# The last operations of the rope tables take a scratch unit of their own late in the first feed-forward stage; in the closing norm the third tile's weight and scale go to GpSimd and ScalarE

## The chip, the cores and the metric

The kernel runs on one core of one Trainium2 chip. Its engines are TensorE (PE in the profile, its weight loads PEld), VectorE (DVE), ScalarE (ACT), GpSimd (POOL) and SyncE (SP, which here only issues DMAs). Time is device microseconds of one execution; a result is the median of several.

## What is computed

One decoder layer over 512 tokens of width 1024, in float32: half a SwiGLU feed-forward, a mixing block, half a second SwiGLU, and a final RMSNorm.

```python
x = x + 0.5 * swiglu(rms_norm(x, ffn1_norm), ffn1_w_gate, ffn1_w_up, ffn1_w_down)
u = rms_norm(x, mix_norm) @ w_in           # [c_q | c_kv | k_rope | moba q | moba k | moba v]
a_out = mla_attention(c_q, c_kv, k_rope, positions, ...)    # uses apply_rope
b_out = moba_attention(mq, mk, mv, positions)
x = x + concat(a_out, b_out) @ w_out
x = x + 0.5 * swiglu(rms_norm(x, ffn2_norm), ffn2_w_gate, ffn2_w_up, ffn2_w_down)
return rms_norm(x, final_norm)

def apply_rope(x, pos):
    ang = pos[:, :, None, None] * 10000.0 ** (-arange(16) * 2 / 32)
    cos, sin = cos(ang), sin(ang)
    return concat([x1 * cos - x2 * sin, x1 * sin + x2 * cos])
```

[...] The feed-forward's inner width is 2816.

## The kernel before

**The matrix products.** A float32 product is made of three TensorE passes over operands that are split into a high and a low part. Every 512 KB piece of weights that a DMA brings into a buffer `raw` is split by one ACT operation (L251, the high part, a copy) and one DVE operation (L252, the low part, a difference) into two slots of the big tile `ar`. The gate and up matrices of a feed-forward are walked in pairs of column blocks (`pair`, L491). A pair is seven products of 24 matmuls each (`product`, L475, matmuls on L485), made by a scheme that trades one block product for sums of blocks; for this some pieces are first added or subtracted on DVE into the tile `sq` (L292, L295, L300) or in place (L297). Between the products ACT copies banks of PSUM to scratch (L495), and DVE adds them up and multiplies (L511, L513, L516, L517, L522, L524, L527); two silus run on ACT (L514, L525). The seventh product of a pair goes on in the bank that L516 reads after the fifth, so TensorE waits for L516 there. `pump` keeps the splitting up to four products ahead.

**Where the order comes from.** Each engine works its own queue strictly in order. The program is written once, and a scheduler decides the order in each engine's queue: it may put an instruction ahead of others where only data and buffers tie it. It works with durations of its own, not with measured ones. Two helpers shape it: `scr`, a scratch tile cut in nine units that `ualloc` and `ufreeit` hand out in rotation (an instruction that writes a unit must wait for the last reader of its earlier contents), and `aside`, a list of generators that `tick` advances by a step or two after each product, so that side work is written between the products.

**The rope tables.** `rope_tables` (L781) is such a generator, started with the fourth pair of the first feed-forward. It takes one scratch unit and cuts it in eight pieces of 64 columns (`a, t2, t1, n, p, q, z, y`). Some fifty small GpSimd operations on 128x64 (L794 to L849, each three-term step as L787 and L788) reduce the angles; L852 clamps the result in place in `a`. Then the generator idles until `state["late"]`, which is set for the last two of the pairs. After that come |a| on DVE (L857), pi/2 - |a| on GpSimd (L859), three sines on ACT (L862, L864 for the cosines, L866 for the sine of `a`), and a negated copy of the sines on GpSimd (L868). The tables are needed much later, in the mixing block (`c_evac`, L969, and `rope_transpose`, L874).

**The tail.** The last part is a loop over the four 128-token tiles `t` (L1423): the last products of the second half of the columns (L1417), the add to the residual on DVE (L1430), the sum of squares on ACT (L1434), an inverse square root in small steps (L1441 on ACT; L1442 to L1446 on DVE, giving `y`), and the scaling of both halves of the tile by `y` and the final norm's weights `gB`. The left half has been multiplied by its weights on GpSimd earlier (L1409) and is scaled on ACT (L1449); the right half is multiplied by both in one DVE operation (L1453). The last tile, t = 3, is cut in 384 and 128 columns, gets its weights early (L1439), and is scaled on DVE (L1451). SP issues the DMA of the right half (L1454), ACT's queue that of the left (L1455). The tiles `x_69` to `x_72` in the listings are t = 0 to 3.

Of the kernel before, what the change touches and what calls it, by code (L numbers as in the profile page):

```python
# [14 lines left out]
AF = mybir.ActivationFunctionType  # L15
OP = mybir.AluOpType
# [24 lines left out]
def _cut(v):  # L41
    b = np.array([v], np.float32).view(np.uint32) & 0xfffff000
    return float(b.view(np.float32)[0])
# [9 lines left out]
def layer_kernel(ctx, tc, xt, xtok, pos_row, pos_tok, gains, fin, consts, w, wc, out):  # L53
    nc = tc.nc
    V, A, G, T = nc.vector, nc.scalar, nc.gpsimd, nc.tensor
# [90 lines left out]
    def ualloc():  # L146
        u = ufree.popleft()
        return u, scr[:, u * 512:(u + 1) * 512]

    def ufreeit(u):  # L150
        ufree.append(u)
# [627 lines left out]
    blk = scr[:, (NU - 1) * 512:].rearrange("p (t c) -> p t c", t=4)  # L779

    def rope_tables():  # L781
        u, sc = ualloc()
        tl = [sc[:, i * 64:i * 64 + 64] for i in range(8)]
        a, t2, t1, n, p, q, z, y = tl

        def STT(o, a_, c, b_, op0, op1):
            G.tensor_scalar(y, a_, c, 1.0, op0=op0, op1=OP.mult)  # L787
            G.tensor_tensor(o, y, b_, op=op1)  # L788

        pf = sm[:, 68:72]  # L790
        V.tensor_copy(pf, pi)
        yield 1
        v3 = a.rearrange("p (t f) -> p t f", t=4)
        G.tensor_tensor(v3, pf[:, :, None].to_broadcast([128, 4, 16]),  # L794
                        cst[:, None, CINV - C0:CINV - C0 + 16].to_broadcast([128, 4, 16]), op=OP.mult)
        yield 1

        def reduce(x):
            G.tensor_scalar(n, x, 1.0 / _P, MAGIC, op0=OP.mult, op1=OP.add)
            yield 1  # L800
            G.tensor_scalar(n, n, -MAGIC, 1.0, op0=OP.add, op1=OP.mult)
            yield 1
            for c in (PI_A, PI_B, PI_C):
                STT(x, n, -c, x, op0=OP.mult, op1=OP.add)
                yield 1

        def fold(t, x, step):

            d = math.fmod(step, _P)
            d = d - _P if d > math.pi else d  # L810
            da = _cut(d)
            db = _cut(d - da)
            dc = d - da - db
            G.tensor_scalar(n, t, da / step / _P, MAGIC, op0=OP.mult, op1=OP.add)
            yield 1
            G.tensor_scalar(n, n, -MAGIC, 1.0, op0=OP.add, op1=OP.mult)
            yield 1
            G.tensor_scalar(x, t, da / step, 1.0, op0=OP.mult, op1=OP.mult)
            yield 1
            STT(x, n, -PI_A, x, op0=OP.mult, op1=OP.add)  # L820
            yield 1
            STT(x, t, db / step, x, op0=OP.mult, op1=OP.add)
            yield 1
            STT(x, n, -PI_B, x, op0=OP.mult, op1=OP.add)
            yield 1
            STT(x, t, dc / step, x, op0=OP.mult, op1=OP.add)
            yield 1
            STT(x, n, -PI_C, x, op0=OP.mult, op1=OP.add)
            yield 1

        m2, m1 = MAGIC * 2.0 ** 21, MAGIC * 2.0 ** 12
        G.tensor_scalar(t2, a, m2, 1.0, op0=OP.add, op1=OP.mult)
        yield 1
        G.tensor_scalar(t2, t2, -m2, 1.0, op0=OP.add, op1=OP.mult)
        yield 1
        G.tensor_tensor(a, a, t2, op=OP.subtract)
        yield 1
        G.tensor_scalar(t1, a, m1, 1.0, op0=OP.add, op1=OP.mult)
        yield 1
        G.tensor_scalar(t1, t1, -m1, 1.0, op0=OP.add, op1=OP.mult)  # L840
        yield 1
        G.tensor_tensor(a, a, t1, op=OP.subtract)
        yield 1
        yield from reduce(a)
        yield from fold(t1, p, 2.0 ** 12)
        yield from fold(t2, q, 2.0 ** 21)
        G.tensor_tensor(p, p, q, op=OP.add)
        yield 1
        G.tensor_tensor(a, a, p, op=OP.add)  # L849
        yield 1  # L850
        yield from reduce(a)
        G.tensor_scalar(a, a, 3.1415925, -3.1415925, op0=OP.min, op1=OP.max)  # L852
        yield 1

        while not state["late"]:
            yield 1
        V.scalar_tensor_tensor(z, a, -1.0, a, op0=OP.mult, op1=OP.max)  # L857
        yield 1
        G.tensor_scalar(z, z, -1.0, math.pi / 2, op0=OP.mult, op1=OP.add)  # L859
        yield 1  # L860
        z3 = z.rearrange("p (t f) -> p t f", t=4)
        A.activation(blk[:, :, 64:80], z3, AF.Sin)  # L862
        yield 1
        A.activation(blk[:, :, 80:96], z3, AF.Sin)  # L864
        yield 1
        A.activation(blk[:, :, 112:128], v3, AF.Sin)  # L866
        yield 1
        G.tensor_scalar(blk[:, :, 96:112], blk[:, :, 112:128], -1.0, 1.0, op0=OP.mult, op1=OP.mult)  # L868
        yield 1
        G.memset(blk[:, :, 0:64], 1.0)  # L870
        yield 1
        ufreeit(u)
# [8 lines left out]
    def dist_tables():  # L881
# [30 lines left out]
        for i in range(4):  # L912
# [10 lines left out]
            yield 1  # L923

    gate_up(c_f1, c_s1, start_mid0, start_mid1, rope_tables)
    down(c_d1, 8)
    close_part()
# [471 lines left out]
    gB = tabs[:, 0:1024]  # L1399
# [7 lines left out]
    for t in range(4):  # L1407
        xs = X[t][:, 0:512]
# [6 lines left out]
    def tail_mm(c, t, n):  # L1415
        a, b = parts[t][n]
        ts = slice(t * 128, t * 128 + 128)  # L1417
        ws = slice(512 + a, 512 + b)
        mm3(banks[acc[t][n]][:, 0:b - a], hi_(hT[c])[:, ts], lo_(hT[c])[:, ts],
            whi(c)[:, ws], wlo(c)[:, ws], t == 3 and c == last[0], c == last[-1],  # L1420
            skip_group_check=True)

    for t in range(4):  # L1423
        u, xg = ualloc()
        v = v0[:, t:t + 1]
        for n, (a, b) in enumerate(parts[t]):
            for c in last:
                tail_mm(c, t, n)
            xs = X[t][:, 512 + a:512 + b]
            V.scalar_tensor_tensor(xs, banks[acc[t][n]][:, 0:b - a], rh[:, t:t + 1], xs,  # L1430
                                   op0=OP.mult, op1=OP.add)
            uj, junk = ualloc()
            s1 = ss[:, 2 * t + n:2 * t + n + 1]
            A.activation(junk[:, 0:b - a], xs, AF.Square, accum_out=s1)  # L1434
            ufreeit(uj)
            if n + 1 < len(parts[t]):
                V.scalar_tensor_tensor(v, s1, 1.0 / D, v, op0=OP.mult, op1=OP.add)
            if t == 3:
                V.tensor_tensor(xg[:, a:b], xs, gB[:, 512 + a:512 + b], op=OP.mult)  # L1439
        w1, w2, y, z = tv[:, t:t + 1], tv[:, 4 + t:5 + t], rstd[:, t:t + 1], tt[:, t:t + 1]  # L1440
        A.activation(w1, s1, AF.Sqrt, scale=1.0 / D, bias=v)  # L1441
        V.scalar_tensor_tensor(w2, s1, 1.0 / D, v, op0=OP.mult, op1=OP.add)  # L1442
        V.tensor_scalar(w2, w2, -0.5, None, op0=OP.mult)
        V.reciprocal(y, w1)
        V.scalar_tensor_tensor(z, y, y, w2, op0=OP.mult, op1=OP.mult)
        V.scalar_tensor_tensor(y, z, 1.5, y, op0=OP.add, op1=OP.mult)  # L1446
        o = out[t * 128:t * 128 + 128, :]
        xs = X[t][:, 0:512]
        A.activation(xs, xs, AF.Copy, scale=y)  # L1449
        if t == 3:  # L1450
            V.tensor_scalar(xg, xg, y, None, op0=OP.mult)  # L1451
        else:
            V.scalar_tensor_tensor(xg, X[t][:, 512:1024], y, gB[:, 512:1024], op0=OP.mult, op1=OP.mult)  # L1453
        nc.sync.dma_start(o[:, 512:1024], xg)  # L1454
        nc.scalar.dma_start(o[:, 0:512], xs)  # L1455
# [88 lines left out]
```

## Time and profile before

| | |
|---|---|
| median of 3 runs | 953.11 us (951.67 to 954.19) |
| the profiled execution | 952.19 us, span 950.4 us, mean granted TensorE clock 0.989 |
| PE busy | 920.2 us, 97% |
| PEld busy | 838.1 us, 88% |
| DVE busy | 748.6 us, 79% |
| ACT busy | 517.4 us, 54% |
| POOL busy | 116.7 us, 12% |

The profile is of one execution. Its time, 952.19 us, holds the span from the first to the last instruction and 1.8 us around it. A row of a timeline gives the start in us from the span's start, the duration, the engine, the line, the operation, what is written and read, and in brackets the idle time before it with what ended it. In the rows of groups, "busy, mean ns" stand behind the bar. A sequencer's row (SPq, ACTq) is the issue of a DMA. `scr`, `sm`, `ar`, `sq`, `raw`, `bank`, `x`, `tabs` are the tiles; `tabs` holds `gB` in the tail.

### The profile page before, as it was taken

Reading aid. Unit: us, or ns where it says so; the run is one execution under the profiler, and the core shown is the slowest. Engines: PE = TensorE matmul, PEld = TensorE weight load, DVE = VectorE, ACT = ScalarE, POOL = GpSimd, SP = SyncE. Lnnn points to the kernel's source line nnn. Section 1 sums busy time; section 2 is a strip of 40 time slices with the busy share of each in tenths; the row PEclk is TensorE's granted clock in tenths of the full one; section 3 lists DMA queues with packets and bytes.
Section 4 is the critical chain, followed back from the end, with each engine's and each line's share of the span. In section 5 each row is a group of like instructions: output and inputs, shape, how many; then the busy total and the mean of one; then the engine's idle time right before and its main releaser. Section 6 shows DMA issues by size and latency. Waiting matters only on the chain.

```text
span 950.4 us, 15102 instructions
## 1 busy us (share of the span) xinstructions
PE 920.2 (97%) x5901; PEld 838.1 (88%) x5901; DVE 748.6 (79%) x1090; ACT 517.4 (54%) x832; POOL 116.7 (12%) x173
## 2 busy tenths in 40 slices
PE   8993999999999999999999999999999999999997
PEld 6993999999988888998787888899999999988886
DVE  6984989879988956445688887689798879988845
ACT  7643544545636525455787865655455544735524
POOL 2053000000000000011756730000000000000001
PEclk9997999999999999999999999999999999999999
DMA  9420433224603424132434362123233323610302
GB/s 329 174 89 24 133 112 112 90 91 152 220 5 100 118 89 138 62 126 72 152 121 152 125 195 98 45 69 109 90 93 127 114 89 112 221 67 26 109 0 89
DMA packets 38088, 105.41 MB, mean 111 GB/s; under 512 B 4480, under 2 KB 11264, under 8 KB 38016
## 3 DMA queue, kind: packets, MB, share of 16 engines
q1 hardware_dynamic: 37008, 102.61, 33.2%
q10 hardware_dynamic: 1008, 1.84, 0.5%
q8 instruction: 46, 0.75, 0.3%
q14 instruction: 26, 0.21, 0.1%
HBM read 90.40 MB, written 2.10 MB: 97 GB/s over the span
## 4 chain that ended last, share of the span: by engine, by line
PE 46%; ACT 2%; DVE 1%; POOL 1%; DMA 1%; issue 0%; ACTq 0%; SPq 0%; DVEq 0%; POOLq 0%
PE bank L485 21%; PE bank L326 7%; PE bank L328 7%; PE bank L327 7%; PE bank L1190 2%; PE bank L1172 1%; POOL scr L1143 1%; ACT scr L1135 1%; DMA ext<-scr 0%; PE bank L402 0%; ACT ar L251 0%; DMA ar<-scr 0%; DVE ext L1176 0%; ACT ar L1175 0%; POOL ext L1259 0%
## 5 line engine op out<-in xcount | busy, mean ns | idle before, releaser
L485 PE MATMUL bank<-ar 128*128 128x256 f32 x3360 | 406.6, 284 | 16.6 <-DVE scr L516 16.0
L485 PEld LDWEIGHTS bank<-ar 128*128 128x128 f32 x3360 | 405.2, 193 | 17.7 <-DVE scr L516 16.4
L251 ACT ACTIVATE ar<-raw 128x1024 fp32r<-128x1024 f32 (+3 forms) x182 | 177.0, 982 | 155.3 <-issue 45.5
L326 PE MATMUL bank<-ar 128*128 128x512 f32 (+4 forms) x664 | 255.3, 385 | 2.6 <-ACT ar L251 2.2
L328 PE MATMUL bank<-ar 128*128 128x512 f32 (+4 forms) x664 | 253.7, 382 | 0.0
L327 PE MATMUL bank<-ar 128*128 128x512 f32 (+4 forms) x664 | 253.6, 382 | 0.0
L252 DVE TENSOR_TENSOR ar<-raw,ar 128x1024 fp32r<-128x1024 f32 (+2 forms) x164 | 192.0, 1181 | 53.9 <-ACT ar L251 35.8
L326 PEld LDWEIGHTS bank<-ar 128*128 128x128 f32 x664 | 124.8, 188 | 25.9 <-ACT ar L251 2.6
L328 PEld LDWEIGHTS bank<-ar 128*128 128x128 f32 x664 | 125.1, 188 | 23.3
L327 PEld LDWEIGHTS bank<-ar 128*128 128x128 f32 x664 | 125.2, 188 | 22.4 <-DVE ar L390 0.2
L251 ACT ACTIVATE ar<-sq 128x1024 fp32r<-128x1024 f32 x62 | 65.6, 1058 | 77.4 <-DVE sq L295 27.1
L252 DVE TENSOR_TENSOR ar<-sq,ar 128x1024 fp32r<-128x1024 f32 x62 | 75.6, 1220 | 26.8 <-ACT ar L251 26.8
L1409 POOL TENSOR_TENSOR x<-x,tabs 128x512 f32<-128x512 f32 x4 | 5.2, 1288 | 353.6 <-ACT scr L354 353.6
L1143 POOL TENSOR_SCALAR scr<-scr,sm 128x128 f32<-128x128 f32 (+1 forms) x64 | 41.1, 662 | 41.4 <-DVE sm L1140 40.5
L617 DVE SCALAR_TENSOR_TENSOR x<-bank,sm,x 128x512 f32<-128x512 f32 x37 | 27.0, 747 | 23.8 <-PE bank L328 23.8
L1135 ACT ACTIVATE scr<-scr,sm 128x256 f32<-128x256 f32 (+1 forms) x64 | 35.3, 553 | 16.9 <-DVE sm L1127 16.8
L495 ACT ACTIVATE scr<-bank 128x512 f32<-128x512 f32 x60 | 34.9, 581 | 6.7 <-PE bank L485 6.7
L354 ACT ACTIVATE scr<-x 128x512 f32<-128x512 f32 x28 | 17.5, 631 | 29.2 <-DVE x L617 27.0
L948 POOL MEMSET ext<- 64x512 f32 x6 | 3.3, 547 | 215.0 <-DVE ar L252 214.5
L575 ACT ACTIVATE ar<-h 128x512 fp32r<-128x512 f32 x28 | 17.3, 630 | 17.1 <-PE bank L327 8.8
L252 POOL TENSOR_TENSOR ar<-raw,ar 128x512 fp32r<-128x512 f32 x18 | 24.1, 1351 | 9.2 <-ACT ar L251 8.3
L295 DVE TENSOR_TENSOR sq<-sq,raw 128x1024 f32<-128x1024 f32 x20 | 24.5, 1223 | 0.5
(239 smaller groups left out, 926.8 us busy)
## 6 DMA issues: line engine op xcount, KB each, us to landing
raw<-in_w_dram SPq DMA_DIRECT2D x144, 512.0 KB, 3.5
h<-in_w_dram SPq DMA_DIRECT2D x8, 512.0 KB, 3.5
ext<-scr SPq DMA_DIRECT2D x13, 256.0 KB, 2.4
raw<-in_wc_dram SPq DMA_DIRECT2D x8, 336.0 KB, 3.3
ext<-scr SPq DMA_DIRECT2D x13, 192.0 KB, 2.3
x<-in_xtok_dram SPq DMA_DIRECT2D x4, 512.0 KB, 8.2
ext<-scr SPq DMA_DIRECT2D x16, 128.0 KB, 2.1
xs<-in_xt_dram SPq DMA_DIRECT2D x5, 256.0 KB, 5.0
```

The costliest lines, as they stand in the source:

```text
L251: A.activation(sl(h)[:, a:b], src[:, a:b], AF.Copy)
L252: (e or V).tensor_tensor(sl(l)[:, a:b], src[:, a:b], slf(h)[:, a:b], op=OP.subtract)
L295: V.tensor_tensor(sq, sq, r(q11), op=OP.subtract)
L326: T.matmul(ps, lhsT=ah, rhs=bh, start=start, stop=False, **kw)
L327: T.matmul(ps, lhsT=ah, rhs=bl, start=False, stop=False, **kw)
L328: T.matmul(ps, lhsT=al, rhs=bh, start=False, stop=stop, **kw)
L485: T.matmul(o, lhsT=a_[:, ws], rhs=b_[:, xs_], start=first and e == 0 and k == 0 and n == 0, stop=k == 3 and n == 2, skip_group_check=True)
L495: A.activation(t, banks[b], AF.Copy)
L617: V.scalar_tensor_tensor(xs, banks[b], r, xs, op0=OP.mult, op1=OP.add)
L1135: A.activation(p, p, AF.Exp, scale=-1.0, bias=mn[z][:, i:i + 1], accum_out=rs[z][:, i:i + 1])
L1143: G.tensor_scalar(p, p, ri[z][:, i:i + 1], 1.0, op0=OP.mult, op1=OP.mult)
L1190: T.matmul(banks[b][:, 128 * j:512], lhsT=vw, rhs=pr[:, o:o + n], start=(j == 0 and e == 0), stop=(j == 3 and e == 1))
```

## The change

Two edits. In the rope tables, the piece `z` of the generator's unit is no longer used, and nothing after the idling stands in that unit: once `late` is set, a second unit is taken, with two pieces `e` and `z`. The clamp moves behind the idling and writes `e`; |e| goes to `z` on DVE as before; pi/2 - z moves from GpSimd to DVE; the sine of the angles reads `e`. The second unit is given back after the three sines. In the tail, for t = 2 the right half's weight is multiplied on GpSimd right after the add to the residual, the right half is scaled by `y` on ACT, the left half by `y` on GpSimd, and SP issues both DMAs.

```diff
-        a, t2, t1, n, p, q, z, y = tl
+        a, t2, t1, n, p, q, _, y = tl
...
         yield from reduce(a)
-        G.tensor_scalar(a, a, 3.1415925, -3.1415925, op0=OP.min, op1=OP.max)
-        yield 1
 
         while not state["late"]:
             yield 1
-        V.scalar_tensor_tensor(z, a, -1.0, a, op0=OP.mult, op1=OP.max)
-        yield 1
-        G.tensor_scalar(z, z, -1.0, math.pi / 2, op0=OP.mult, op1=OP.add)
-        yield 1
-        z3 = z.rearrange("p (t f) -> p t f", t=4)
+        u2, sc = ualloc()
+        e, z = sc[:, 0:64], sc[:, 64:128]
+        e3, z3 = (x.rearrange("p (t f) -> p t f", t=4) for x in (e, z))
+        G.tensor_scalar(e, a, 3.1415925, -3.1415925, op0=OP.min, op1=OP.max)
+        yield 1
+        V.scalar_tensor_tensor(z, e, -1.0, e, op0=OP.mult, op1=OP.max)
+        yield 1
+        V.tensor_scalar(z, z, -1.0, math.pi / 2, op0=OP.mult, op1=OP.add)
+        yield 1
         A.activation(blk[:, :, 64:80], z3, AF.Sin)
         yield 1
         A.activation(blk[:, :, 80:96], z3, AF.Sin)
         yield 1
-        A.activation(blk[:, :, 112:128], v3, AF.Sin)
-        yield 1
+        A.activation(blk[:, :, 112:128], e3, AF.Sin)
+        yield 1
+        ufreeit(u2)
...
-            if t == 3:
-                V.tensor_tensor(xg[:, a:b], xs, gB[:, 512 + a:512 + b], op=OP.mult)
+            if t > 1:
+                (G if t == 2 else V).tensor_tensor(xg[:, a:b], xs, gB[:, 512 + a:512 + b], op=OP.mult)
...
         xs = X[t][:, 0:512]
+        if t == 2:
+
+            A.activation(xg, xg, AF.Copy, scale=y)
+            G.tensor_scalar(xs, xs, y, 1.0, op0=OP.mult, op1=OP.mult)
+            nc.sync.dma_start(o[:, 512:1024], xg)
+            nc.sync.dma_start(o[:, 0:512], xs)
+            continue
         A.activation(xs, xs, AF.Copy, scale=y)
```

How the scheduler's order changes is seen at three places. The first is ACT's queue in the second pair of the first feed-forward, as the difference (a minus stands before the rows of before alone). L866 is the sine of the angles, L495 a copy from PSUM, L251 a high part, L514 a silu.

```order
 L251 ACTIVATE ar<-raw_63 128x1024
 L495 ACTIVATE scr<-bank_87 128x512
-L866 ACTIVATE scr<-scr 128x4x16
 L251 ACTIVATE ar<-sq 128x1024
 L514 ACTIVATE scr<-scr 128x512
```

Before, the sine stood here, long before `late`, because only its input tied it; now nothing of the rope tables stands here.

The second is ACT's queue in the last pairs of the same stage, of the changed kernel. L868, L864 and L866 are there the lines of the three sines (of `e`, and the two of `z`).

```order
L525 ACTIVATE scr<-scr 128x512
L251 ACTIVATE ar<-raw_63 128x1024
L495 ACTIVATE scr<-bank_81 128x512
L868 ACTIVATE scr<-scr 128x4x16
L864 ACTIVATE scr<-scr 128x4x16
L495 ACTIVATE scr<-bank_88 128x512
L251 ACTIVATE ar<-raw_64 128x1024
L866 ACTIVATE scr<-scr 128x4x16
L251 ACTIVATE ar<-sq 128x1024
```

The three sines now stand together here, and the copy of `bank_88` ahead of the high part of `raw_64`, which it followed before.

The third is DVE's queue at the same place, as the difference. In the changed kernel L860 is |e| and L862 pi/2 - z; L587 and L588 (and L589, a few rows on) are sums for the down projection.

```order
 L252 TENSOR_TENSOR ar<-raw_63,ar 128x1024
-L252 TENSOR_TENSOR ar<-raw_64,ar 128x1024
-L252 TENSOR_TENSOR ar<-sq,ar 128x1024
+L860 SCALAR_TENSOR_TENSOR scr<-scr 128x64
+L862 TENSOR_SCALAR scr<-scr 128x64
+L252 TENSOR_TENSOR ar<-raw_64,ar 128x1024
+L587 TENSOR_TENSOR scr<-h_3_95 128x512
+L588 TENSOR_TENSOR h_3_95<-h_3_95,h_4_96 128x2x256
+L252 TENSOR_TENSOR ar<-sq,ar 128x1024
+L589 TENSOR_TENSOR scr<-h_3_95 128x512
 L295 TENSOR_TENSOR sq<-sq,raw_64 128x1024
```

The two operations of the rope tables stand ahead of the low part of `raw_64`, and three sums have come forward from a later pair. TensorE's own queue is the same in both kernels.

## The prediction

> **What bounds the kernel now.** I read the page first: its slices show where TensorE, the bound at 97% of the span, isn't working.
>
> ```profile
> PE   8993999999999999999999999999999999999997
> POOL 2053000000000000011756730000000000000001
> PEclk9997999999999999999999999999999999999999
> ```
>
> A slice is 23.76 us. The fourth, 71 to 95 us, has TensorE busy for three tenths, and nowhere else does it fall below eight before the tail. GpSimd's first busy stretch stands just ahead. So I asked who waited for whom between 40 and 110 us (total, times, longest), and then for the engines' rows in order of time.
>
> ```profile
> ACT scr L866 <- POOL scr L852: 20.1, 1, 20.1
> PE bank L485 <- DVE scr L516: 16.0, 2, 15.1
> DVE ar L252 <- ACT ar L251: 15.0, 1, 15.0
> ```
>
> ```profile
> 53.80 17.18 PE L485 MATMUL bank<-ar 128*128 128x256 f32 x141 [0.85 <-DVE scr L516]
> 62.26 0.60 ACT L495 ACTIVATE scr<-bank 128x512 f32<-128x512 f32 x1 [0.70 <-PE bank L485]
> 67.90 1.34 DVE L297 TENSOR_TENSOR raw<-raw,raw 128x1024 f32<-128x1024 f32 x1
> 69.43 0.32 POOL L788 TENSOR_TENSOR scr<-scr 128x64 f32<-128x64 f32 x1
> 82.71 0.24 POOL L852 TENSOR_SCALAR scr<-scr 128x64 f32<-128x64 f32 x1
> 82.98 0.26 ACT L866 ACTIVATE scr<-scr 128x64 f32<-128x64 f32 x1 [20.13 <-POOL scr L852]
> 83.15 1.04 ACT L251 ACTIVATE ar<-sq 128x1024 fp32r<-128x1024 f32 x1
> 84.22 1.23 DVE L252 TENSOR_TENSOR ar<-sq,ar 128x1024 fp32r<-128x1024 f32 x1 [14.97 <-ACT ar L251]
> 85.36 0.69 DVE L516 TENSOR_TENSOR scr<-bank,scr 128x512 f32<-128x512 f32 x1
> 86.10 24.09 PE L485 MATMUL bank<-ar 128*128 128x256 f32 x187 [15.12 <-DVE scr L516]
> ```
>
> It is one chain. The sine L866 stands in ACT's queue at 62.86 us, and its input comes out of GpSimd's long chain only at 82.95. Behind it waits the high part L251; for that waits DVE's L252; behind that, in DVE's queue, stands L516, and TensorE, which ended at 53.80 + 17.18 = 70.98, waits for L516 until 86.10. A sine that nobody needs for 200 us stops the kernel for 15.1 us. The stretches show what else goes with it (columns: length, then busy us and instructions of PE, PEld, DVE, ACT, POOL, then granted clock, DMA share, GB/s).
>
> ```profile
> 55.50:69.20 13.70, 13.70 (x116) 13.70 (x116) 13.70 (x14) 5.51 (x7) 12.54 (x14) 1.00 0.47 154
> 69.20:83.20 14.00, 1.78 (x15) 1.57 (x14) 0.04 (x1) 0.21 (x2) 10.64 (x39) 0.73 0.00 1
> 86.00:89.00 3.00, 2.90 (x13) 2.90 (x14) 3.00 (x5) 1.06 (x1) 0.00 (x0) 0.50 0.17 20
> 89.00:92.00 3.00, 3.00 (x26) 3.00 (x25) 2.32 (x3) 1.46 (x2) 0.00 (x0) 0.96 0.38 154
> 100.00:200.00 100.00, 100.00 (x835) 100.00 (x835) 87.09 (x91) 49.87 (x62) 1.06 (x1) 1.00 0.34 109
> ```
>
> After the stop the granted clock is 0.50 for 3 us, in which 13 matmuls run and not 26.
>
> **The change, part by part. The early stop.** L866 leaves its early place. ACT then takes the high part as soon as `sq` is written; DVE had done that before L297 began, so ACT ends at 67.90 + 1.04 = 68.94 at the latest. DVE is free of L297 at 67.90 + 1.34 = 69.24, which now comes last. All of DVE's rows from L252 on move up by 84.22 - 69.24 = 14.98, so L516 ends at 85.36 + 0.69 - 14.98 = 71.07. TensorE, done at 70.98, waits some 0.15 us in place of 15.12: gain 15.0. The DMAs, at 1 GB/s while everything stood, had filled their buffers, so they are no limit at that point.
>
> **The clock.** With a wait of 0.15 us I expect no drop: the one of 0.85 us at 53.80 is followed by a stretch at 1.00. The 13 matmuls missing in 86 to 89 are worth half of 3 us: gain 1.5.
>
> **GpSimd beside DVE.** The stop had a use: GpSimd ran 39 small operations in 14 us beside an idle DVE. Now they run beside a busy one. How that goes, 55.5 to 69.2 shows: 14 operations in 13.7 us, 0.98 each, so the 39 take 38 us and end near 107, on nobody's path before `late`. What they cost DVE, the same difference L252 shows, first in that stretch, then between 110 and 200 us where GpSimd is idle:
>
> ```profile
> L252 DVE TENSOR_TENSOR ar<-raw,ar 128x1024 fp32r<-128x1024 f32 x4 | 5.0, 1286 | 0.0
> L252 DVE TENSOR_TENSOR ar<-raw,ar 128x1024 fp32r<-128x1024 f32 x20 | 24.3, 1220 | 4.1 <-ACT ar L251 4.1
> 102.13 0.69 DVE L511 TENSOR_TENSOR scr<-bank,scr 128x512 f32<-128x512 f32 x1 [1.18 <-PE bank L485]
> 105.87 0.68 DVE L516 TENSOR_TENSOR scr<-bank,scr 128x512 f32<-128x512 f32 x1
> ```
>
> That is 66 ns on 1220, 5%; over DVE's 15 us of work from 69.24 up to the next L511 up to 0.8 us. Before, DVE waited 1.18 us for TensorE there (102.13); TensorE now comes 1.5 us earlier against DVE, so DVE is behind by 0.3 + 0.8 = 1.1. From L511's start to the next L516's end DVE took 106.55 - 102.13 = 4.4; TensorE has two products of 24 matmuls in between, at 3/26 us each 5.5. The margin of 1.1 just covers it. Lowest cost 0; highest, if each of the 39 held DVE for its own 10.64/39 = 0.27 us, 10.6, less the 12.9% of 43 us that DVE idles (87.09 of 100): 5. It is nearest to the measured stretch; I take a loss of 0.4.
>
> The Trainium skill (SBUF — State Buffer, Who interferes with whom) says that a DVE instruction with two SBUF inputs and a GpSimd instruction that reads SBUF exclude each other, the later one blocking fully. By that rule alone the loss would be the 5 us. The 66 ns here fall well short of it, as if most of the blocking fell on GpSimd.
>
> **The late place.** What arrives there are five small operations: the clamp on GpSimd, idle since 107; DVE's two; three sines on ACT, half busy.
>
> ```profile
> 99.91 1.15 POOL L859 TENSOR_SCALAR scr<-scr 128x64 f32<-128x64 f32 x1 [16.34 <-DVE scr L857]
> 177.91 1.23 DVE L252 TENSOR_TENSOR ar<-raw,ar 128x1024 fp32r<-128x1024 f32 x1 [1.48 <-ACT ar L251]
> 180.85 1.23 DVE L252 TENSOR_TENSOR ar<-sq,ar 128x1024 fp32r<-128x1024 f32 x1 [1.71 <-ACT ar L251]
> ```
>
> DVE idles 1.48 and 1.71 us right where L860, L862 and two of the three sums now stand (0.2 each for the small ones, 0.7 for a sum): covered, with about 0.6 us left over against a margin of 1.1. Behind L860, should it wait, stand the low parts for the next products, and TensorE for those. The clamp's unit was last used more than a pair before, since seven units rotate and a pair takes three; so no wait: 0. The price of pi/2 - z on DVE isn't in the trace; between 0.15 (a small operation) and the 1.15 of L859 both fit the gap.
>
> **The tail.**
>
> ```profile
> 940.06 0.75 DVE L1430 SCALAR_TENSOR_TENSOR x<-bank,sm,x 128x512 f32<-128x512 f32 x1
> 940.92 0.75 DVE L1453 SCALAR_TENSOR_TENSOR scr<-x,sm,tabs 128x512 f32<-128x512 f32 x1
> 943.74 0.75 DVE L1453 SCALAR_TENSOR_TENSOR scr<-x,sm,tabs 128x512 f32<-128x512 f32 x1
> 943.80 0.72 ACT L1449 ACTIVATE x<-x,sm 128x512 f32<-128x512 f32 x1 [0.36 <-DVE sm L1446]
> 944.48 0.34 DVE L1430 SCALAR_TENSOR_TENSOR x<-bank,sm,x 128x128 f32<-128x128 f32 x1
> 944.55 0.35 ACTq L1455 DMA_DIRECT2D out_dram<-x  x1
> 944.94 0.31 ACT L1434 ACTIVATE scr<-x 128x128 f32<-128x128 f32 x1 [0.42 <-DVE x L1430]
> 947.16 0.34 ACTq L1455 DMA_DIRECT2D out_dram<-x  x1
> L1409 POOL TENSOR_TENSOR x<-x,tabs 128x512 f32<-128x512 f32 x4 | 5.2, 1288 | 353.6 <-ACT scr L354 353.6
> L1143 POOL TENSOR_SCALAR scr<-scr,sm 128x512 f32<-128x512 f32 x16 | 13.7, 856 | 0.0
> 542.22 1.58 DVE L1208 TENSOR_TENSOR ar<-scr,ar 128x512 fp32r<-128x512 f32 x1 [0.36 <-ACT ar L1207]
> 540.70 2.55 POOL L252 TENSOR_TENSOR ar<-raw,ar 128x512 fp32r<-128x512 f32 x2 [3.53 <-ACT ar L251]
> ```
>
> Everything up to the last DMA's issue at 947.16 hangs on the last tile's L1430 and L1434. With L1453 of t = 2 gone from DVE, L1430 starts 0.66 earlier; ACT, busy with t = 2's scale until 944.52 but without the issue behind it, starts L1434 at 944.5 instead of 944.94: gain 0.45. GpSimd's scale (0.86 by L1143) ends near 944.7 and SP issues after it, well ahead of the last tile's. Against it stands GpSimd's weight, 1.29 by L1409, from 940.9: just when L1453 of t = 1 starts at 940.92. At 542.22 a DVE operation of 0.69 us took 1.58 beside GpSimd's difference, done when that was over. If GpSimd comes first here, L1453 ends at 942.8 and not 941.67, the last tile's chain behind it is 0.8 late at `y`, and L1434 starts at 945.25: loss 0.3. Should DVE come first, GpSimd's 1.29 begins at 941.7 and holds up the last tile's weight by 0.25: gain 0.2. The two starts lie within 0.02 us; between +0.45 and -0.3 I take 0.
>
> By that section of the Trainium skill whichever starts first keeps the other out; by it the tail gives -0.3 or +0.2, never +0.45. The 1.58 agrees with it.
>
> **The sum.** 15.0 + 1.5 - 0.4 + 0 = 16.1. All durations are of the profiled execution, 952.19 us with what lies around its span: 952.19 - 16.1 = 936.1. The median of the runs shown lies 0.92 above it, so the median comes to 953.11 - 16.1 = 937.0.
>
> **The rivals.** (1) *DVE becomes the bound behind the stop*: it was continuously busy from 84 to 101, which speaks for it; if it can't follow TensorE at full clock, the 1.5 is lost and another 1 beside it: 953.11 - 13.6 = 939.5. (2) *GpSimd's chain blocks DVE in full*, 5 in place of 0.4: 941.6. The 1286 ns row speaks against it. (3) *The wait moves to the late place and is longer*: L860 stands in DVE's queue, near 176.4 - 16.5 = 160 us, for a clamp that ends the GpSimd chain. With 16.1 gained and 3.2 of idle time there, it is slower than before if the chain ends after 160 + 19.3 = 179, which takes 110/39 = 2.8 us an operation; at 3.0 (end at 186) it is 26 - 3.2 = 23 lost, 960. Measured are 0.98. (4) *It doesn't do it*: a sine still waits early, 953. The order shows none there.
>
> **How the numbers follow.** Forecast 0.76, (1) 0.14, (2) 0.07, (3) 0.02, (4) 0.01. A measurement of this kernel tells 0.3%, 2.9 us, from no change; forecast, (1) and (2) lie beyond it: faster 0.97, same 0.01, slower 0.02. The range goes down to 937.0 less the tail's 0.45, the 0.4 and the runs' spread of 1.4, 934.8; up to (1) with half of that spread, 940.2. It leaves out (2) to (4) and the edges of the forecast, under 0.2.
>
> **What would show it.** Right: no wait of PE over 1 us between 60 and 100 us, granted clock 1.00 in every 3 us there, GpSimd's chain ending near 107, DVE's L252 near 1290 ns meanwhile, the three sines near 160 us with no wait before L860. Wrong: a wait of L485 for DVE or ACT of several us in 69 to 110; DVE's rows beside GpSimd at 1.5 us; a new wait near 160. For the tail: L1434 of 128 columns against the last L1430 of 384 columns, 2.77 us later before, 2.3 with the full gain, and whether L1453 of t = 1 takes 0.75 or 1.9.

## The result, and the profile after

| | before | after |
|---|---|---|
| median of 4 runs | 952.75 us (951.67 to 954.19) | 935.72 us (935.00 to 937.47) |
| the profiled execution | 952.19 us, span 950.4 | 937.47 us, span 935.7 |
| mean granted clock | 0.989 | 0.997 |

The ratio of the runs is 0.9824, interval 0.9812 to 0.9836: 17 us faster, 1.3 us beyond the forecast of 937.0 and within its range. The profiled execution is the slowest of the four; what it holds more than that of the first experiment comes up under "GpSimd and DVE in the mixing block" below.

The page's slices after: the hole in the fourth slice is gone, the clock's digit there is 9 instead of 7, and GpSimd's first busy stretch now reaches into the fifth.

```profile
PE   8999999999999999999999999999999999999996
POOL 2059401000000000013666530000000000000002
PEclk9999999999999999999999999999999999999998
```

The rows in order of time at the place of the old stop (start, duration, engine, line; in brackets the idle time ahead):

```profile
53.88 58.32 PE L485 MATMUL bank<-ar 128*128 128x256 f32 x481 [0.85 <-DVE scr L516]
67.98 1.34 DVE L297 TENSOR_TENSOR raw<-raw,raw 128x1024 f32<-128x1024 f32 x1
67.50 1.06 ACT L251 ACTIVATE ar<-sq 128x1024 fp32r<-128x1024 f32 x1 [4.57 <-DVE sq L292]
69.24 1.25 DVE L252 TENSOR_TENSOR ar<-sq,ar 128x1024 fp32r<-128x1024 f32 x1
70.42 0.68 DVE L516 TENSOR_TENSOR scr<-bank,scr 128x512 f32<-128x512 f32 x1
70.76 0.24 POOL L787 TENSOR_SCALAR scr<-scr 128x64 f32<-128x64 f32 x1
71.15 0.38 PE L485 MATMUL bank<-ar 128*128 128x256 f32 x1
102.97 1.17 POOL L788 TENSOR_TENSOR scr<-scr 128x64 f32<-128x64 f32 x1
```

TensorE's row now runs over 481 matmuls without a wait of its own. ACT has the high part done at 67.50 + 1.06 = 68.56, while DVE is still in L297; DVE goes from L297 straight into L252 and L516, and the matmul that started at 86.10 before starts at 71.15. GpSimd's chain ends at 102.97 + 1.17 = 104.14. The same by stretches (length, then busy us and instructions of PE, PEld, DVE, ACT, POOL, granted clock, DMA share, GB/s), and the low parts' durations in the stretch from 69.2 us to the chain's end:

```profile
69.00:72.00 3.00, 2.91 (x25) 2.70 (x24) 3.00 (x4) 1.15 (x2) 2.75 (x4) 1.00 0.00 0
69.20:104.20 35.00, 34.91 (x291) 34.70 (x290) 34.55 (x36) 19.16 (x23) 31.92 (x38) 1.00 0.32 106
```

```profile
L252 DVE TENSOR_TENSOR ar<-raw,ar 128x1024 fp32r<-128x1024 f32 x8 | 10.1, 1285 | 0.0
```

TensorE idles 0.09 us in all of it (3.00 less 2.91, and 35.00 less 34.91), at a clock of 1.00. DVE is busy for 34.55 of 35.00 us: it keeps up, with 0.45 us to spare. GpSimd's 38 operations take 0.92 us apiece from 69.2 on (35 over 38), and L252 takes 1285 ns.

The late place, in the listing of after:

```profile
157.74 1.21 DVE L297 TENSOR_TENSOR raw<-raw,raw 128x1024 f32<-128x1024 f32 x1
157.98 2.21 POOL L858 TENSOR_SCALAR scr<-scr 128x64 f32<-128x64 f32 x1 [53.84 <-DVE h L527]
158.87 1.22 DVE L252 TENSOR_TENSOR ar<-raw,ar 128x1024 fp32r<-128x1024 f32 x1
160.22 0.26 ACT L868 ACTIVATE scr<-scr 128x64 f32<-128x64 f32 x1 [1.03 <-POOL scr L858]
160.22 0.22 DVE L860 SCALAR_TENSOR_TENSOR scr<-scr 128x64 f32<-128x64 f32 x1
162.43 1.23 DVE L252 TENSOR_TENSOR ar<-raw,ar 128x1024 fp32r<-128x1024 f32 x1 [1.75 <-ACT ar L251]
```

The clamp did wait: for L527 of the pair that had just ended, the last reader of the unit that the clamp writes, and then it took 2.21 us, over DVE's L297 and L252. This is not yet the place of `late`: L527 runs four more times in this stage (at 176.04, 197.45, 216.87 and 236.38), and `late` is set for the last two pairs. The scheduler has moved the clamp, and what hangs on it, up to where its unit became free, two pairs ahead of where it is written. The clamp ended at 160.19, and DVE, free at 158.87 + 1.22 = 160.09, waited 0.13 for it. All of this stands in time that DVE has: before L252 at 162.43 it idles 1.75 us for ACT. TensorE waits for nothing there.

The tail of after (its lines: L1433 the add, L1437 the squares, L1442 the weight, L1463 the right half's scale on DVE):

```profile
925.99 1.30 POOL L1442 TENSOR_TENSOR scr<-x,tabs 128x512 f32<-128x512 f32 x1 [6.15 <-DVE sm L1449]
926.01 1.82 DVE L1463 SCALAR_TENSOR_TENSOR scr<-x,sm,tabs 128x512 f32<-128x512 f32 x1
928.00 0.61 DVE L1433 SCALAR_TENSOR_TENSOR x<-bank,sm,x 128x384 f32<-128x384 f32 x1
928.20 0.28 PE L328 MATMUL bank<-ar 128*128 128x128 f32 x1
930.25 0.29 ACT L1437 ACTIVATE scr<-x 128x128 f32<-128x128 f32 x1
```

GpSimd's weight starts 0.02 us ahead of DVE's scale of t = 1, and that scale takes 1.82 us in place of 0.75. From the last matmul's end, 928.48, to the span's end, 935.7, it is 7.2 us; before, with the last matmul as below, it was 950.4 - 943.42 = 7.0. The tail has become 0.2 us longer.

```profile
943.14 0.28 PE L328 MATMUL bank<-ar 128*128 128x128 f32 x1
```

### The profile page after: what moved, and what is told of

It is laid out like the page before. It is cut to its first block, busy times and chain, and to the rows that moved or that the text cites. A ratio compares the mean times of both kernels' runs of the same rounds, so it can differ in the third digit from the quotient of the medians.

```text
span 935.7 us, 15101 instructions
## 1 busy us (share of the span) xinstructions
PE 918.8 (98%) x5901; PEld 835.7 (89%) x5901; DVE 752.2 (80%) x1090; ACT 517.5 (55%) x832; POOL 140.8 (15%) x174
## 4 chain that ended last, share of the span: by engine, by line
PE 46%; ACT 3%; DVE 2%; issue 1%; DMA 0%; POOL 0%; DVEq 0%; ACTq 0%; POOLq 0%
PE bank L485 22%; PE bank L326 7%; PE bank L328 7%; PE bank L327 7%; PE bank L1193 2%; ACT scr L1138 1%; PE bank L1175 1%; ACT ar L251 0%; DVE ext L1179 0%; PE bank L402 0%; POOL scr L1146 0%; DVE scr L1463 0%; DMA ar<-scr 0%; ACT ar L1178 0%; ACT scr L1202 0%
## 5 line engine op out<-in xcount | busy, mean ns | idle before, releaser
L251 ACT ACTIVATE ar<-raw 128x1024 fp32r<-128x1024 f32 (+3 forms) x182 | 176.9, 982 | 148.6 <-issue 42.9
L252 DVE TENSOR_TENSOR ar<-raw,ar 128x1024 fp32r<-128x1024 f32 (+2 forms) x164 | 192.3, 1182 | 53.7 <-ACT ar L251 35.6
L251 ACT ACTIVATE ar<-sq 128x1024 fp32r<-128x1024 f32 x62 | 65.7, 1059 | 86.0 <-DVE sq L295 27.0
L252 DVE TENSOR_TENSOR ar<-sq,ar 128x1024 fp32r<-128x1024 f32 x62 | 75.8, 1222 | 10.2 <-ACT ar L251 10.2
L495 ACT ACTIVATE scr<-bank 128x512 f32<-128x512 f32 x60 | 34.9, 581 | 6.3 <-PE bank L485 6.3
L252 POOL TENSOR_TENSOR ar<-raw,ar 128x512 fp32r<-128x512 f32 x18 | 23.6, 1322 | 9.2 <-ACT ar L251 8.3
L297 DVE TENSOR_TENSOR raw<-raw,raw 128x1024 f32<-128x1024 f32 x20 | 24.5, 1225 | 0.2
```

The lines of the kernel that those rows point to most:

```text
L251: A.activation(sl(h)[:, a:b], src[:, a:b], AF.Copy)
L252: (e or V).tensor_tensor(sl(l)[:, a:b], src[:, a:b], slf(h)[:, a:b], op=OP.subtract)
L297: V.tensor_tensor(r(q21), r(q11), r(q21), op=OP.subtract)
L495: A.activation(t, banks[b], AF.Copy)
```

## The experiments

The theory: the whole gain is the one sine that waited early in ACT's queue, 15 us of stop and 1.5 us of clock; GpSimd's chain beside the busy DVE costs TensorE nothing; the tail costs 0.2 us, by the lock of GpSimd's weight against DVE's scale. Against it stood that the tail carries part of the gain, that the chain costs something that the profile of after hides, and that the way the last operations are shared out matters.

**The rope tables alone.** The changed kernel with the tail of before.

```diff
-            if t > 1:
-                (G if t == 2 else V).tensor_tensor(xg[:, a:b], ...)
+            if t == 3:
+                V.tensor_tensor(xg[:, a:b], ...)
...
-        if t == 2:
-            A.activation(xg, xg, AF.Copy, scale=y)
-            G.tensor_scalar(xs, xs, y, 1.0, op0=OP.mult, op1=OP.mult)
...
```

> The rope tables' edit alone, with the tail of before. Theory (the early sine held ACT, DVE and TensorE for 15.0 us and cost 1.4 us of slow clock behind it; the tail's edit costs 0.25): the whole gain is here, 952.5 - 16.4 = 936.1 or less, within 0.5 us of the changed kernel, and from the last matmul to the end of the span 6.98 us as before, not the 7.22 of the changed kernel. Rival (the tail's edit brings a part of the gain): slower than the changed kernel by 0.5 us or more, with a tail longer than 7.22.

Measured: 935.81 us (935.05 to 936.30), ratio 0.9824, 0.9809 to 0.9839; the profiled execution 935.46. The tail's rows:

```profile
924.23 0.75 DVE L1456 SCALAR_TENSOR_TENSOR scr<-x,sm,tabs 128x512 f32<-128x512 f32 x1
925.45 0.62 DVE L1433 SCALAR_TENSOR_TENSOR x<-bank,sm,x 128x384 f32<-128x384 f32 x1 [0.18 <-PE bank L328]
926.42 0.28 PE L328 MATMUL bank<-ar 128*128 128x128 f32 x1
928.22 0.31 ACT L1437 ACTIVATE scr<-x 128x128 f32<-128x128 f32 x1 [0.42 <-DVE x L1433]
```

The whole gain is here. The last squares start 928.22 - 926.70 = 1.52 us after the last matmul's end, as before (944.94 - 943.42), where in after it is 930.25 - 928.48 = 1.77.

**The tail alone.** Before, with the tail of after.

```diff
-            if t == 3:
-                V.tensor_tensor(xg[:, a:b], ...)
+            if t > 1:
+                (G if t == 2 else V).tensor_tensor(xg[:, a:b], ...)
...
+        if t == 2:
+            A.activation(xg, xg, AF.Copy, scale=y)
+            G.tensor_scalar(xs, xs, y, 1.0, op0=OP.mult, op1=OP.mult)
...
```

> The kernel before with the tail's edit alone. Theory (the tail's edit costs 0.25 us, since VectorE's scale of t = 1 and GpSimd's weight of t = 2 exclude each other): the time within 0.3% of before, 952.9; from the last matmul to the end of the span 7.2 us and not 6.98; the scale of t = 1 takes 1.8 us; TensorE still stops for 15.1 us at 71 us. Rival (the tail's edit gains 0.45): 6.5 us from the last matmul to the end.

Measured: 953.32 us against 952.52 of before (10 and 13 runs), ratio 1.0006, 0.9997 to 1.0016. One of its ten runs took 3136.32 us, the other nine 952.30 to 955.65; what happened in that one is not known. In the profile the same lock:

```profile
944.16 1.30 POOL L1439 TENSOR_TENSOR scr<-x,tabs 128x512 f32<-128x512 f32 x1 [6.12 <-DVE sm L1446]
944.18 1.83 DVE L1460 SCALAR_TENSOR_TENSOR scr<-x,sm,tabs 128x512 f32<-128x512 f32 x1
946.41 0.28 PE L328 MATMUL bank<-ar 128*128 128x128 f32 x1
948.43 0.29 ACT L1434 ACTIVATE scr<-x 128x128 f32<-128x128 f32 x1
```

From the last matmul's end to the last squares 948.43 - 946.69 = 1.74, and to the span's end, 953.9, 7.2. The tail's edit is worth no gain; its loss of 0.2 us is seen in the trace and is too small for the times.

**The weight a little later.** The changed kernel, with a one-column copy on GpSimd that ties the weight of t = 2 behind DVE's scale of t = 1.

```diff
+        before = xg if t else None
         u, xg = ualloc()
...
+            if t == 2:
+                G.tensor_scalar(xg[:, 0:1], before[:, 0:1], 1.0, 1.0, op0=OP.mult, op1=OP.mult)
```

> The changed kernel, but GpSimd's weight of t = 2 waits until VectorE's scale of t = 1 has ended (a GpSimd copy of one column of that result into the column that the weight then overwrites ties them). Theory (GpSimd's weight and VectorE's scale of t = 1, both with two inputs in SBUF, exclude each other): the scale of t = 1 takes 0.75 us again and not 1.82; GpSimd's weight then holds up the last tile's weight of 384 columns, so about half is given back, and the last tile's sum of squares of 128 columns starts 1.5 us after the last matmul, not 1.77. Rival (the scale was slow for another reason, such as the bank or the queue): it stays at 1.8. In time either way within 0.5 us of the changed kernel.

Measured: 935.16 us (934.77 to 935.68), ratio 0.9820, 0.9803 to 0.9836.

```profile
923.62 0.75 DVE L1466 SCALAR_TENSOR_TENSOR scr<-x,sm,tabs 128x512 f32<-128x512 f32 x1
924.81 1.28 POOL L1445 TENSOR_TENSOR scr<-x,tabs 128x512 f32<-128x512 f32 x1
925.49 1.02 DVE L1445 TENSOR_TENSOR scr<-x,tabs 128x384 f32<-128x384 f32 x1
925.81 0.28 PE L328 MATMUL bank<-ar 128*128 128x128 f32 x1
926.92 0.72 ACT L1457 ACTIVATE scr<-scr,sm 128x512 f32<-128x512 f32 x1 [0.82 <-DVE sm L1441]
927.55 0.29 ACT L1438 ACTIVATE scr<-x 128x128 f32<-128x128 f32 x1
```

The scale of t = 1 is back at 0.75, and the last squares start 927.55 - 926.09 = 1.46 us after the last matmul. The lock is now paid at the last tile's weight, 1.02 us for an operation of 0.56, and the squares wait for ACT, which scales t = 2 until 927.64. Of the 0.45 us that the tail could have given, 0.06 is left against 1.52. It is the lowest median of all, 0.56 below after, but its interval and that of after lie over each other: a version that is at least as good, not one shown to be better.

**The sine of the angles back in the first unit.** The changed kernel, with the clamp and that one sine as before; |a| reads the first unit again too.

```diff
+        G.tensor_scalar(a, a, 3.1415925, -3.1415925, op0=OP.min, op1=OP.max)
+        yield 1
         while not state["late"]:
             yield 1
...
-        G.tensor_scalar(e, a, 3.1415925, -3.1415925, op0=OP.min, op1=OP.max)
-        yield 1
-        V.scalar_tensor_tensor(z, e, -1.0, e, op0=OP.mult, op1=OP.max)
+        V.scalar_tensor_tensor(z, a, -1.0, a, op0=OP.mult, op1=OP.max)
...
-        A.activation(blk[:, :, 112:128], e3, AF.Sin)
+        A.activation(blk[:, :, 112:128], v3, AF.Sin)
```

> The changed kernel, but the clamp stands in the first unit before the idling and the sine of the angles and |a| read it there, as before; the cosines' pieces stay in the late unit. Theory (what stops the kernel is that one sine's place in ACT's queue, which only its input decides): the sine goes back behind the second pair's third copy, ACT waits some 20 us for GpSimd, TensorE 15 us from 71 us, the clock drops behind it: about 952, as before. Rival (the cosines' steps or the move of pi/2 - z to VectorE matter): between 936 and 950.

Measured: 952.55 us (951.18 to 954.43), ratio 0.9999, 0.9989 to 1.0010. Who waits, between 40 and 110 us:

```profile
ACT scr L868 <- POOL scr L852: 20.1, 1, 20.1
PE bank L485 <- DVE scr L516: 15.9, 2, 15.1
```

All that the change gained hangs on where this one sine stands, and with it the clamp that feeds it. The second unit, pi/2 - z on DVE and the tail are in this kernel too, and bring nothing.

**The folds twice.** The changed kernel, with both folds of the angles done two times over: 26 more GpSimd operations, so that the chain runs longer beside the busy DVE.

```diff
-        yield from fold(t1, p, 2.0 ** 12)
-        yield from fold(t2, q, 2.0 ** 21)
+        for _ in range(2):
+            yield from fold(t1, p, 2.0 ** 12)
+            yield from fold(t2, q, 2.0 ** 21)
```

> The changed kernel with both folds of the angles done twice, each writing the same values again: 26 more small GpSimd operations in the chain, beside a busy VectorE, ending near 125 us and not 104. Theory (the chain now lies off every path, and costs VectorE some 30 to 60 ns an operation, inside its slack): no change, within 0.3%, and no wait of TensorE in 60 to 130 us. Rival (each GpSimd operation holds VectorE for its own 0.27 us): 26 x 0.27 = 7.0 us less the slack of 2.5, 4.5 us slower than the changed kernel.

Measured: 935.49 us (934.83 to 937.21), ratio 0.9824, 0.9809 to 0.9839. The chain's end, with DVE beside it, and the stretch up to it:

```profile
122.65 0.32 POOL L788 TENSOR_TENSOR scr<-scr 128x64 f32<-128x64 f32 x1
124.11 1.41 POOL L788 TENSOR_TENSOR scr<-scr 128x64 f32<-128x64 f32 x1
124.11 1.23 DVE L252 TENSOR_TENSOR ar<-sq,ar 128x1024 fp32r<-128x1024 f32 x1 [1.65 <-ACT ar L251]
```

```profile
69.20:125.50 56.30, 56.19 (x468) 55.99 (x468) 53.57 (x55) 29.34 (x35) 51.17 (x64) 1.00 0.34 113
```

The chain ends at 125.5 instead of 104.1, and TensorE is busy for 56.19 of 56.30 us. The load lasts 21 us longer and still TensorE has no wait, so that the single load costs nothing does not hang on a slack that a longer chain would use up.

**The chain cut short.** Before, without the folds and one of the two last reductions (the tables then don't hold the reference's angles). The sine waits early still, but for a shorter chain.

```diff
         G.tensor_tensor(a, a, t1, op=OP.subtract)
-        yield 1
-        yield from reduce(a)
-        yield from fold(t1, p, 2.0 ** 12)
-        yield from fold(t2, q, 2.0 ** 21)
-        G.tensor_tensor(p, p, q, op=OP.add)
-        yield 1
-        G.tensor_tensor(a, a, p, op=OP.add)
         yield 1
         yield from reduce(a)
```

> The kernel before, with the first reduction and both folds of the angles left out, so that 17 of the 52 small GpSimd operations are left; the rest, the early sine too, as before. Its tables do not hold the reference's angles. The scheduler puts the sine two rows earlier in ACT's queue, ahead of the third copy from PSUM of the second pair, so TensorE stops after the fourth product, near 65.1 us, and not after the sixth. Theory (the sine holds ACT until GpSimd's chain ends, and everything behind it): the chain ends near 70 us, TensorE goes on near 71 and is where it was at 86.1 by 76.5, so the kernel gains some 9.5 us: 943. Rival (the stop is of a fixed length, or comes from the sine or its function table itself): within 2 us of before.

Measured: 940.79 us (940.45 to 941.47), ratio 0.9877, 0.9863 to 0.9892, a gain of 11.7 us. The rows at the stop, and stretches of 1.5 us behind it:

```profile
67.10 0.24 POOL L845 TENSOR_SCALAR scr<-scr 128x64 f32<-128x64 f32 x1
67.37 0.26 ACT L859 ACTIVATE scr<-scr 128x64 f32<-128x64 f32 x1 [6.29 <-POOL scr L845]
68.17 10.03 PE L485 MATMUL bank<-ar 128*128 128x256 f32 x69 [3.54 <-ACT scr L495]
```

```profile
68.00:69.50 1.50, 1.33 (x10) 1.34 (x11) 1.35 (x2) 0.11 (x1) 0.00 (x0) 0.93 0.00 0
69.50:71.00 1.50, 1.50 (x9) 1.50 (x8) 1.50 (x3) 0.94 (x1) 0.00 (x0) 0.50 0.00 0
71.00:72.50 1.50, 1.50 (x9) 1.50 (x8) 1.50 (x2) 0.64 (x2) 0.00 (x0) 0.50 0.00 0
74.00:75.50 1.50, 1.50 (x14) 1.50 (x14) 1.23 (x2) 0.78 (x1) 0.00 (x0) 1.00 0.00 0
```

The stop's length goes with the chain's end: 15.12 us has become 3.54, and 15.12 - 3.54 = 11.6 is the gain. The clock's part hasn't gone with it: two stretches at a clock of 0.50 hold 9 matmuls each, where 14 stand in the one at 1.00, so it is paid as after the long stop. What the expectation had otherwise is taken up below.

**pi/2 - z back on GpSimd.** The changed kernel, with the second of the two late operations of DVE, the argument of the sines that give the cosines, where it was.

```diff
-        V.tensor_scalar(z, z, -1.0, math.pi / 2, op0=OP.mult, op1=OP.add)
+        G.tensor_scalar(z, z, -1.0, math.pi / 2, op0=OP.mult, op1=OP.add)
```

> The changed kernel, but pi/2 - z goes back to GpSimd, in the late unit. Theory (the late place has slack on every engine): within 0.3% of the changed kernel, 935.7; ACT waits 1 to 2 us longer for the cosines' sine, and TensorE waits for nothing more there. Rival (the move of this step to VectorE is a part of the gain): slower by 1 us or more.

Measured: 935.74 us (934.99 to 936.14), ratio 0.9825, 0.9808 to 0.9841.

```profile
160.37 0.24 POOL L862 TENSOR_SCALAR scr<-scr 128x64 f32<-128x64 f32 x1
160.64 0.26 ACT L864 ACTIVATE scr<-scr 128x64 f32<-128x64 f32 x1 [0.56 <-POOL scr L862]
```

ACT waits 0.56 us for this sine (0.23 for DVE's result in after; 1 to 2 us more had been expected), and TensorE for nothing. This part of the change makes no difference.

## Why the prediction was right, point by point

**The early stop: 15.0, measured 14.95** (86.10 - 71.15). The chain of four waits was read rightly, and what came last behind it, DVE's L297 and then L252 and L516, was named rightly; TensorE's wait of 0.15 came out as 0.09. The sine put back alone brings all of it back.

**The clock: 1.5, measured 1.4.** By the start of each matmul, the distance between the two traces grows from 14.95 at 71.15 us to 16.34 fourteen matmuls on, and then stands.

**GpSimd beside DVE: a loss of 0.4, measured 0.** Of its two bounds, 0 and 5, the lower one holds. The inputs were right, 1285 ns for L252 against 1286 read from the stretch before the stop, 0.92 us for one of GpSimd's operations against 0.98, the end at 104 against 107. What failed is the step from DVE's loss to TensorE's: DVE has 0.45 us to spare in 35, and with twice the folds no wait appears either, so the rivals that DVE becomes the bound or that it is blocked in full have no place. The cited section of the Trainium skill (SBUF — State Buffer, Who interferes with whom) has the later of two such instructions block fully. The runs agree as to GpSimd, whose 0.24 to 0.32 us operations take 1.1 to 1.2 beside a busy DVE and fall back to 0.24 and 0.32 where DVE waits (122.65 above, in DVE's 1.65 us of waiting up to 124.11). They also run in full beside the DVE operations that read one of their inputs from a PSUM bank (L511, L516, L522, L527): in after, the eight that began there between 69.2 and 104.2 us took 0.24 to 0.33 (70.76 above is one), while of the 29 that began beside DVE operations with both inputs in SBUF 22 took over 1 us. That the price stays with GpSimd fits its being nearly always the later one here, which no row shows directly.

**The late place: 0, measured 0, for a reason that was wrong.** "The clamp's unit was last used more than a pair before" holds for the order in which the program is written, where two whole pairs lie between; but the scheduler moved the clamp up to just behind the unit's last reader, L527 of the pair just ended. So it waited for that, and then took 2.21 us, 0.1 us past the end of the second of two DVE operations of 1.2 us each. That it cost nothing is due to DVE's idle time there, which the prediction had found as well: a wait of 0.13 against 1.75. The rival of a longer wait at the late place needed a chain that ends after 179 us; it ended at 104.

**The tail: 0 between +0.45 and -0.3, measured -0.2.** The lock named there is what happened, in all five kernels that have the weight at this place, with GpSimd 0.02 us ahead each time (after and the tail alone are shown). The sign that the prediction named for the full gain misled: the last squares start 930.25 - 928.00 = 2.25 us after the last tile's first add, and 2.3 was to mean a gain. Both ends had moved: that add itself starts 0.48 us before the last matmul's end, and with the tail of before, in the first experiment, 1.25 before it. A distance must be taken from an event that the edit can't move, such as the last matmul.

**The sum.** 14.95 + 1.4 - 0.2 = 16.1, the number forecast. That the two sums agree to a tenth is in part luck: the loss of 0.4 that did not come makes up for the tail's 0.2 and for what the clock and the early stop fell short. The profiled execution of after shows 952.19 - 937.47 = 14.7, and the first experiment's 952.19 - 935.46 = 16.7; the last section tells of the difference between them, of which only the tail's 0.2 is the edit's. The medians lie 17.0 apart, 952.75 against 935.72; half an interval of the ratio is 1.1 us, so the 0.9 between that and the sum can't be told from nothing.

**The shortened chain: 2.2 us more than expected.** The expectation took the stop that is left over for longer. The chain's last steps run at 0.24 to 0.32 us once DVE stands still, and in the shorter chain most of the rest had passed before the stop. The scheduler also put the sine one place earlier in ACT's queue, ahead of the copy L495, so the stop that is left has another last link (TensorE waits for L495, not for L516). With the sine where it had been, behind that copy, the chain's end at 67.34 would have been ahead of L297's end at 69.24; this was not tried.

## What to carry to other kernels

Where a scheduler may put an instruction anywhere between its input and its use, an instruction that nobody needs yet can stop an engine that works its queue in order; give its input a buffer that only becomes free late, and it moves: here not to where it is written, but to just behind the last reader of that buffer. Read such a stop as a chain from the engine that idles back to the one instruction that nobody waits for, and then ask what is late next: here it was DVE, 0.1 us behind. A slow chain on GpSimd beside a full DVE cost nothing here while its results were not wanted, but one large GpSimd operation of 1.30 us that starts just ahead of a DVE operation on the last path made that operation take 1.82 us instead of 0.75.

## What the runs showed of the hardware that was not expected

**GpSimd and DVE in the mixing block.** The profiled executions of after and of the first experiment lie 2.0 us apart, though the change between them is in the tail. By the starts of the matmuls 0.5 us of it are there before the first 34 us are over, 0.2 are the tail's, and the rest, 1.3, arises just behind one place, where GpSimd's difference L252 and DVE's L1278 start together. After, then the rope tables alone, the same instructions in the same order (GpSimd's row joins two differences, and the second is the one meant):

```profile
509.89 2.55 POOL L252 TENSOR_TENSOR ar<-raw,ar 128x512 fp32r<-128x512 f32 x2
511.17 1.83 DVE L1278 TENSOR_TENSOR ext<-scr,ext 128x512 fp32r<-128x512 f32 x1
```

```profile
509.26 3.11 POOL L252 TENSOR_TENSOR ar<-raw,ar 128x512 fp32r<-128x512 f32 x2
510.53 0.68 DVE L1278 TENSOR_TENSOR ext<-scr,ext 128x512 fp32r<-128x512 f32 x1
```

In after DVE takes 1.83 us, so GpSimd went first; in the other DVE takes 0.68, and GpSimd's second difference 1.86 in place of 1.30. In all nine profiles of this case GpSimd's record starts first, by 6 to 23 ns, and yet DVE went first in six (before among them) and GpSimd in three (after, the tail alone, the folds twice). Measured against the first experiment or before, the matmuls that follow fall back by 1.1 to 1.3 us in each of the three in which DVE came second. So at such a distance the order of the records doesn't tell who is kept waiting. That runs of one kernel differ by a microsecond for it is likely, but not shown, since each kernel has one profile. The rule of the Trainium skill (SBUF — State Buffer, Who interferes with whom) that the first to issue holds the other up is not contradicted, but it doesn't say who that is here. In the tail, at 21 to 24 ns, GpSimd went first each time.

**The clock's price didn't grow with the stop.** After 15.1 us of standing still, matmul starts lie 0.213 us apart from 86.10 to 89.25 in before and 0.120 from there on; after 3.54 us of it, in the shortened chain, they lie 0.120 apart for the first 1.2 us, then 0.213 from 69.37 to 72.76. Each costs 1.4 us; waits of 0.85 us cost none. The Trainium skill (TensorE: Matmul & The Clock Gate, Part 1: The HAM clock gate) gives about 3.4 us for the work that runs at half the clock after a rest, set by a window that runs free of the matmuls. The 3.2 and 3.4 us here agree, and the slow stretch that begins only 1.2 us after the work has resumed fits a window that isn't tied to the stop.
